# Hybrid decoder layer: gate weights kept for the last pass, output products on VectorE, an earlier reload of h, and a planner that lets short operations go first

## The chip, the cores and the metric

One core of one Trainium2 chip runs the whole layer. The metric is the device time of the execution in microseconds, as the median of several runs. PE is TensorE, DVE VectorE, ACT ScalarE, POOL GpSimd, and SP's queue issues the DMAs.

## The reference

A decoder layer over 1024 tokens of width 1024: an RG-LRU recurrence and a latent attention side by side, an output projection, a SwiGLU feed-forward of width 2816, and a gated per-layer embedding, then a last normalization. The parts that the change touches:

```python
h = h + y @ w_out[l]
vff = rmsnorm(h, g_ffn[l])
h = h + (jax.nn.silu(vff @ w_ffn_gate[l]) * (vff @ w_ffn_up[l])) @ w_ffn_down[l]
e = rmsnorm(p[l] @ w_ple_proj[l], g_ple_post[l])
gate = jax.nn.sigmoid(rmsnorm(h, g_ple_in[l]) @ w_ple_gate[l])
h = h + gate * e
return rmsnorm(h, g_final)
```

## The kernel before

All data is fp32 and transposed: channels lie on the partitions (8 tiles of 128), the 1024 tokens on the free axis. For products a tensor is split into a high and a low fp32r part (`hilo`, `split`, `load_w`: an ACT copy makes the high part, a DVE subtraction the low one), and each product is three matmuls. The feed-forward uses a scheme with seven block products in place of eight (`products`, `PART`), whose sums and differences DVE makes.

The code does not issue instructions as it runs. `Plan` records them; `Plan.order` then plays all engines forward with a table of costs and picks, on each engine that is free, the recorded operation with the smallest key that has its inputs and its buffers. A key is the place in the recording plus shifts (`plan.shift`, `OFF`). Each engine then runs its list strictly in the planned order, so an operation that is late holds all that stand behind it. All instructions are emitted from one line, L364 in the profile.

SBUF is handed out in 51 slots of 128x1024, PSUM in four single banks (`bank`) and two double ones.

The stages, in order: input products and the recurrence (`in_tile`, `rg_front`, `rg_pair`: products `rg`, results `rg_r`, `rg_i`, a scan `rg_h`), attention, the output projection (`wo`), whose result h is kept in DRAM (`hd`). Then 11 pairs of `ff_gate(p)` and `ff_up(p)`, each a block of 84 matmuls of 128x512. `make_x` turns the product of the two into seven hi/lo tiles `hx`, which `spill` stores in DRAM one by one, except for p = 10 (`KEEP`). Then come the down products, in four chunks of the 11 (`CHUNKS`) with four calls of `down` each: `fetch` loads the `hx` tiles back, a call loads two tiles of h in chunk 0, and DVE adds each product to h (`h<-ff_z`, `h<-ff_y`, `h<-ff_x`).

At the end, the embedding products (`ple`), and then the gate products (`gate_mm`, `plg`): 8 tiles n for each of three column ranges h of 512, 256 and 256 tokens (`CH`), 24 matmuls each. `gate_out` evaluates one tile on DVE and ACT (`gt`, `e`, `h`, `o_sq`, `o_acc`), and `out_task` normalizes one column range: transposes `no_ms` and `no_bc`, a short chain on [128, 2 to 4] numbers (`n_m`, `n_rt`, `n_r`, `n_t`), then products of h with `no_rb` and the output DMAs. Each `wpg` weight tile is 512 KB and is loaded and split once for each of the three ranges.

Of the kernel before, what the change touches and what calls it, by code (L numbers as in the profile page):

```python
# [12 lines left out]
ALU = mybir.AluOpType  # L13
# [127 lines left out]
class Plan:  # L141
# [25 lines left out]
    def cost(self, eng, fn, a, k, out):  # L167
        w = out.width() if isinstance(out, View) else 0
        if fn == "dma_start":
            v = k["out"] if isinstance(k["out"], View) else k["in_"]  # L170
            return v.shape[0] * v.width() * 4 / 360e3, 2.1
        if eng == "tensor":
            if fn == "transpose":
                return 0.108, 0.18
            return max(w * 0.000417 + 0.0135, 0.113), 0.18
        if eng == "vector":
            if fn == "reciprocal":
                return 0.065 + w * 0.0063, 0.13
            if fn in ("tensor_reduce", "reduce_sum"):
                return 0.065 + k["in_"].width() * 0.00104, 0.13  # L180
            ptr = 0.061 * any(isinstance(x, View) for x in (k.get("scalar"), *a[2:])) if fn == "scalar_tensor_tensor" else 0.0
            one = fn in ("tensor_copy", "tensor_scalar", "tensor_scalar_mul", "tensor_scalar_add", "tensor_scalar_max")
            if one and all(v.buf.tag not in PS for v in [*a, *k.values()] if isinstance(v, View)):
                return 0.068 + w * 0.00052, 0.13
            return 0.068 + ptr + w * 0.00104, 0.13
        if eng == "scalar":
            src = k["in_"] if "in_" in k else a[1]
            c = (0.052 if src.buf.tag in PS else 0.093) + w * 0.000833
            c += 0.093 * sum(isinstance(k.get(n), View) for n in ("scale", "bias"))
            c += 0.2 * isinstance(k.get("accum_out"), View)  # L190
            return c, 0.14
        return 0.15 + w * (0.0033 if fn == "tensor_copy" else 0.0022), 0.14
# [49 lines left out]
    def order(self):  # L242
# [28 lines left out]
        while left:  # L271
            while frees and frees[0][0] <= t:
                _, _, tag, n = heapq.heappop(frees)
                free[tag] += n
            moved = False
            for e in names:
                while future[e] and future[e][0][0] <= t:
                    _, i, o = heapq.heappop(future[e])
                    heapq.heappush(avail[e], (o.key, i, o))
                if busy[e] > t or not avail[e]:  # L280
                    continue
                pick, skipped, best = None, [], None
                tries = 0
                while avail[e] and tries < 40:
                    i, _, o = heapq.heappop(avail[e])
                    tries += 1
                    ok = all(b.placed or free[b.tag] > min(unplaced(b), RES.get(b.tag, 99)) for b in o.bufs)
                    if ok:
                        key = i
                        if e == "scalar" and o.table and o.table not in SAME.get(table, ()):  # L290
                            key = i + SWITCH
                        if best is None or key < best[0]:
                            if best is not None:
                                skipped.append((best[1], best[2].idx, best[2]))
                            best = (key, i, o)
                        else:
                            skipped.append((i, o.idx, o))
                        if e != "scalar" or key == i:
                            break
                    else:  # L300
                        skipped.append((i, o.idx, o))
                for s in skipped:
                    heapq.heappush(avail[e], s)
                if best is None:
                    continue
                o = best[2]
                moved = True
                start = t
                c = o.cost
                if o.port:  # L310
                    start = max(t, port)
                    port = start + c
                if o.table and o.table not in SAME.get(table, ()):
                    table = FIRST[o.table]
                    c += 1.28
                for b in o.bufs:
                    if b.placed:
                        continue
                    b.placed = True
                    free[b.tag] -= 1  # L320
                    q, d = queue[b.tag], ahead[b.tag]
                    d[b.pos] = True
                    while head[b.tag] < len(q) and d[head[b.tag]]:
                        head[b.tag] += 1
                busy[e] = start + c
                o.end = start + c + o.lat
                o.st = start
                out.append((t, o.idx, o))
                left -= 1
                for b in o.bufs:  # L330
                    b.left -= 1
                    b.done = max(getattr(b, "done", 0.0), start + c + LAT[e, "tensor"] if b.tag in PS and e != "tensor" else o.end)
                    if not b.left:
                        heapq.heappush(frees, (b.done, b.pos, b.tag, 1))
                for s in o.succ:
                    s.npred -= 1
                    r = start + c + (LAT[e, s.eng] if (e, s.eng) in LAT else o.lat)
                    s.ready = max(s.ready, r)
                    if not s.npred:
                        heapq.heappush(future[s.eng], (s.ready, s.idx, s))  # L340
            nxt = [busy[e] for e in names if busy[e] > t and (avail[e] or future[e])]
            nxt += [future[e][0][0] for e in names if future[e] and future[e][0][0] > t]
            if frees:
                nxt.append(frees[0][0])
            nxt = [x for x in nxt if x > t]
            if not left:
                break
            if not nxt:
                raise RuntimeError("the plan does not fit")
            t = min(nxt)  # L350
# [18 lines left out]
FG = ((0, 1), (2, 3), (4, 5), (6, 7))  # L369
TK = 5  # L370
XLATE = 40
NWIDE = 2
PS = ("bank", "wide")
X0 = 0
SWITCH = 150
RES = {'bank': 1, 'slot': 99}


@with_exitstack
def hybrid_layer(ctx, tc, xT, pT, pos, vec, const, const2, w1, wn, wrg, wq, wkv, wo, wg, wu, *rest):  # L380
# [112 lines left out]
    order += [(("wq", 1), wq[1], S)]  # L493
    order += [(("wo", n), wo[n], S) for n in NO]
    order += [(("wpp", k), wpp[k], S) for k in range(2)]
    order += [(("wpg", n, h), wpg[n], S) for h in range(len(CH)) for n in range(8)]
    ready, issued = {}, [0]

    def weight(key, ahead=2):
# [666 lines left out]
    def ff_gate(p):  # L1166
# [3 lines left out]
        def ahead(i):  # L1170
            pump("g", p)
            if i >= 3:
                pump("u", p)
            if p == 0 and i in (0, 3):
                next(nf, None)

# [16 lines left out]
    def ff_up(p, mid):  # L1193
# [3 lines left out]
        def ahead(i):  # L1197
            pump("u", p)
            if i >= 3:
                if p + 1 < NF // 2:  # L1200
                    pump("g", p + 1)
                else:
                    pump("d", 0)
            if p and p - 1 not in KEEP:
                spill(p - 1)
            mid(i)

        def sink(i, ps):
            r, h = PART[i]
# [30 lines left out]
    def fetch(p, i):  # L1240
        t = slot("hx")
        Y.dma_start(out=t, in_=hx[p][i])
        return halves(t.bitcast(F32R))

    def down(c, m, xs, mid, after=None):
        j = 4 * c + m

        def ahead(i):
            pump("d", j)
            if i >= 3:  # L1250
                pump("d", j + 1)
            mid(i)
            if c == 0 and i == 0:
                for n in (2 * m, 2 * m + 1):
                    hs[n] = slot("h")
                    Y.dma_start(out=hs[n], in_=hd[n])

        def sink(i, ps):
            adds = {0: ((0, 0),), 1: ((1, 1),), 2: ((0, 1),), 3: ((0, 1),), 4: ((1, 1),), 5: ((0, 0),), 6: ((1, 0),)}[i]
# [28 lines left out]
    for p in range(NF // 2):  # L1288
        ff_gate(p)
        ff_up(p, (lambda i: first(p - NF // 2 + 4, i)) if p >= NF // 2 - 2 else lambda i: None)  # L1290
    for p in KEEP:
        kept[p] = list(kept[p])


    hg, pacc = [], []
# [43 lines left out]
    ne = rstd_steps(eacc, 1024, "ne", res_)  # L1339
    np_ = rstd_steps(pacc[0], 1024, "np", rps)  # L1340

    def gate_mm(i):
        h, n = divmod(i, 8)
        wh, wl = weight(("wpg", n, h))
        cw = CH[h].stop - CH[h].start
        ps = bank("plg")[:, :cw]
        for k in range(8):
# [7 lines left out]
    def gate_out(i, ps):  # L1355
# [1 line left out]
        cw = CH[h].stop - CH[h].start  # L1357
        t = slot("gt")[:, :cw]
        e, hn = es[n][:, CH[h]], hs[n][:, CH[h]]
        V.scalar_tensor_tensor(out=e, in0=e, scalar=col("g_ple_post", n), in1=res_[0][:, CH[h]],  # L1360
                               op0=ALU.mult, op1=ALU.mult)
        V.tensor_mul(t, ps, rps[0][:, CH[h]])
        A.activation(t, t, AF.Sigmoid)
        if i == 8 * len(CH) - 1:
# [16 lines left out]
    def out_task(h):  # L1381
        res = []
        yield from rstd_part(oaccs[h], 1024, "no", res, h < len(CH) - 1)
        if h < len(CH) - 1:
            for n in range(8):
                hn = hs[n][:, CH[h]]
                G.tensor_mul(hn, hn, res[0])
                Y.dma_start(out=out[n][:, CH[h]], in_=hn)
            return
        cw = CH[h].stop - CH[h].start  # L1390
# [117 lines left out]
```

## Time and profile before

| | |
|---|---|
| median of 3 runs | 1209.58 us (1207.53 to 1210.05) |
| the profiled execution | 1206.05 us |
| its span, first to last instruction | 1204.2 us |
| PE busy | 1164.7 us, 97% |
| DVE busy | 985.5 us, 82% |
| ACT busy | 645.5 us, 54% |
| POOL busy | 250.8 us, 21% |
| mean granted TensorE clock | 0.992 of full speed |

Busy shares are means over stages with different limits. With PE at 97% most of the time can't be moved by an order of instructions; what can is the time in which PE waits, and the time after its last product. A row of the timeline gives the start, the duration, the engine, the operation with out<-in, and in brackets the idle time before it and what ended it. Durations of successive rows overlap a little: the step from start to start is the cost in a row of them.

### The profile page before, as it was taken

The page shows a single profiled execution, that of the slowest core. Times are in us where ns is not written, and L with a number is a line of the kernel's source. Part 1 is how long each engine was busy: PE and PEld are TensorE (multiplying, and loading weights), DVE is VectorE, ACT ScalarE, POOL GpSimd, SP SyncE. Part 2 cuts the span into 40 slices and gives each one's busy share as a digit, 9 for nine tenths or more (in the row PEclk, how much of TensorE's full clock was granted, in tenths as well). Part 3 has the DMA queues.
Part 4 walks back from the last instruction along what each step waited for, and adds up shares of the span by engine and source line. Part 5 has one row for each costly group of instructions (what it writes and reads, how often), then busy time and mean ns, then how long its engine had stood idle before and what let it go on. Part 6 is the DMA issues. An engine that isn't in the chain of part 4 may idle for free.

```text
span 1204.2 us, 15416 instructions
## 1 busy us (share of the span) xinstructions
PE 1164.7 (97%) x5608; PEld 965.5 (80%) x5608; DVE 985.5 (82%) x1486; ACT 645.5 (54%) x1086; POOL 250.8 (21%) x149
## 2 busy tenths in 40 slices
PE   8999999999999999999999999999899999999995
PEld 6788778888878878888888888887687878887894
DVE  7978788888978599988788788876997658776997
ACT  8447868877936354545444454434332214476565
POOL 0001131412102132333213331233000000343042
PEclk9999999999999999999999999999999999999997
DMA  8001100000405142344443445463978773032362
GB/s 339 19 18 35 36 1 1 1 1 1 149 10 192 71 140 71 140 175 161 154 144 136 175 140 175 158 227 146 382 268 283 256 265 133 25 131 88 105 215 84
DMA packets 48252, 158.01 MB, mean 131 GB/s; under 512 B 5424, under 2 KB 8752, under 8 KB 48176
## 3 DMA queue, kind: packets, MB, share of 16 engines
q1 hardware_dynamic: 48176, 157.02, 36.2%
q8 instruction: 44, 0.72, 0.2%
q14 instruction: 32, 0.26, 0.1%
HBM read 111.91 MB, written 45.09 MB: 130 GB/s over the span
## 4 chain that ended last, share of the span: by engine, by line
PE 82%; DVE 10%; ACT 3%; issue 2%; DMA 2%; SPq 0%; DVEq 0%; ACTq 0%
PE ff_z L364 28%; PE ff_y L364 14%; PE ff_x L364 7%; PE plg L364 6%; PE wo L364 5%; PE s L364 4%; PE wn L364 4%; PE av L364 2%; PE tp L364 2%; PE qps L364 2%; DMA wd_r<-in_wd 2%; PE wn_b L364 1%; DVE h L364 1%; PE wn_a L364 1%; PE wo_a L364 1%
## 5 line engine op out<-in xcount | busy, mean ns | idle before, releaser
L364 POOL TENSOR_TENSOR silu<-silu,nf_rb 128x512 f32<-128x512 f32 x77 | 121.5, 1599 | 279.5 <-DVE silu L364 222.0
L364 PE MATMUL ff_z<-hx,wd 128*128 128x512 f32 x528 | 129.8, 393 | 6.1 <-DVE h L364 5.2
L364 PE MATMUL ff_z<-x,wg 128*128 128x512 f32 x528 | 128.5, 391 | 0.2 <-DVE x L364 0.2
L364 PE MATMUL ff_z<-x,wu 128*128 128x512 f32 x528 | 127.1, 390 | 0.9 <-ACT ff_u L364 0.9
L364 PEld LDWEIGHTS ff_z<-hx,wd 128*128 128x128 f32 x528 | 99.4, 189 | 28.7 <-DVE h L364 6.3
L364 PEld LDWEIGHTS ff_z<-x,wu 128*128 128x128 f32 x528 | 99.0, 188 | 22.1 <-ACT ff_u L364 1.4
L364 PEld LDWEIGHTS ff_z<-x,wg 128*128 128x128 f32 x528 | 98.6, 188 | 22.1 <-DVE x L364 0.9
L364 ACT ACTIVATE wd<-wd_r 128x256 fp32r<-128x256 f32 (+2 forms) x64 | 30.0, 492 | 66.5 <-DMA wd_r<-in_wd 28.1
L364 PE MATMUL ff_y<-hx,wd 128*128 128x512 f32 x264 | 65.4, 390 | 0.0
L364 PE MATMUL ff_y<-x,wg 128*128 128x512 f32 x264 | 64.3, 390 | 0.7 <-ACT x L364 0.7
L364 POOL TENSOR_TENSOR p_acc<-p_acc,sq 128x1024 f32<-128x1024 f32 x7 | 18.2, 2595 | 221.4 <-ACT sq L364 221.3
L364 PE MATMUL ff_y<-x,wu 128*128 128x512 f32 x264 | 63.4, 389 | 0.0
L364 DVE TENSOR_TENSOR h<-ff_z,h 128x512 f32<-128x512 f32 x64 | 44.1, 689 | 23.0 <-PE ff_z L364 22.6
L364 PE MATMUL plg<-hg_h,wpg_l 128*128 128x256 f32 (+1 forms) x192 | 61.5, 320 | 1.3 <-DVE wpg_l L364 1.2
L364 PE MATMUL plg<-hg_h,wpg_h 128*128 128x256 f32 (+1 forms) x192 | 61.5, 320 | 0.3 <-ACT np_rb L364 0.3
L364 PE MATMUL plg<-hg_l,wpg_h 128*128 128x256 f32 (+1 forms) x192 | 61.2, 319 | 0.0
L364 ACT ACTIVATE wu<-wu_r 128x512 fp32r<-128x512 f32 x44 | 27.6, 627 | 59.2 <-DVE wu_r L364 28.1
L364 PEld LDWEIGHTS ff_y<-x,wg 128*128 128x128 f32 x264 | 49.4, 188 | 11.5 <-ACT x L364 1.1
L364 PEld LDWEIGHTS ff_y<-hx,wd 128*128 128x128 f32 x264 | 49.8, 189 | 10.5
L364 PEld LDWEIGHTS ff_y<-x,wu 128*128 128x128 f32 x264 | 49.6, 188 | 10.3
L364 ACT ACTIVATE wd<-wd_s 128x256 fp32r<-128x256 f32 (+2 forms) x48 | 23.6, 499 | 63.1 <-DVE wd_s L364 47.8
L364 DVE TENSOR_REDUCE nm<-s 128x1 f32<-128x128 f32 (+3 forms) x64 | 48.1, 752 | 8.7 <-PE s L364 8.1
(407 smaller groups left out, 3060.1 us busy)
## 6 DMA issues: line engine op xcount, KB each, us to landing
hx<-hx SPq DMA_DIRECT2D x140, 512.0 KB, 4.1
wpg_raw<-in_wpg SPq DMA_DIRECT2D x24, 512.0 KB, 3.5
wg_r<-in_wg SPq DMA_DIRECT2D x22, 512.0 KB, 5.5
wu_r<-in_wu SPq DMA_DIRECT2D x22, 512.0 KB, 4.9
wn_raw<-in_wn SPq DMA_DIRECT2D x10, 512.0 KB, 7.1
wo_raw<-in_wo SPq DMA_DIRECT2D x8, 512.0 KB, 4.6
h<-in_xT SPq DMA_DIRECT2D x8, 512.0 KB, 4.4
hd<-h SPq DMA_DIRECT2D x8, 512.0 KB, 2.9
```

The costliest lines, as they stand in the source:

```text
L364: getattr(self.engines[o.eng], o.fn)(*a, **k)
```

## The change

- `order` gets a rule, `HOLD`: on an engine other than PE, where a short operation (cost under 0.25) with a key smaller by over 20 becomes ready within 0.15 us and before the picked operation would end, the engine is left idle until then.
- The planner's cost of `tensor_tensor_scan` on DVE is doubled.
- `spill(p - 1)` is called in `ff_gate(p)`, where it was called in `ff_up(p)`.
- The keys of the `make_x` operations of p = 10 are raised by `KLATE` = 100.
- `reload_h`: the first two tiles of h are loaded in the last `ff_up`, before its sixth product, and those of m + 1 in `down` of m before its fourth, where each was loaded at the start of its own `down`.
- The `wpg` tiles n = 4 to 7 are kept in SBUF from the second column range for the third (`HELD`), with 4 fewer loads and splits.
- `e * g_ple_post * res_` is made once over 1024 columns, where it was made in three pieces.
- The products of h with `no_rb` of the first two column ranges go from POOL to DVE.

```diff
@@ -176,6 +176,8 @@
+            if fn == "tensor_tensor_scan":
+                return 0.068 + w * 0.0021, 0.13
@@ -302,6 +304,12 @@
+                soon = next((r for r, _, x in future[e][:6] if r < t + HOLD and r + 0.05 < t + best[2].cost
+                             and x.cost < 0.25 and x.key + 20 < best[0]), None) if e != "tensor" else None
+                if soon is not None:
+                    heapq.heappush(avail[e], (best[1], best[2].idx, best[2]))
                     continue
@@ -369,10 +377,15 @@
+HOLD = 0.15
+KLATE = 100
+HL = 5
+HAT = 3
+HELD = 4
@@ -493,7 +506,7 @@
-    order += [(("wpg", n, h), wpg[n], S) for h in range(len(CH)) for n in range(8)]
+    order += [(("wpg", n, h), wpg[n], S) for h in range(len(CH)) for n in range(8) if h < 2 or n < HELD]
@@ -1171,6 +1184,8 @@
             pump("g", p)
             if i >= 3:
                 pump("u", p)
+            if p and p - 1 not in KEEP:
+                spill(p - 1)
@@ -1201,9 +1216,9 @@
-            if p and p - 1 not in KEEP:
-                spill(p - 1)
             mid(i)
+            if p == NF // 2 - 1 and i == HL:
+                reload_h(0)
@@ -1242,6 +1257,11 @@
+    def reload_h(m):
+        for n in (2 * m, 2 * m + 1):
+            hs[n] = slot("h")
+            Y.dma_start(out=hs[n], in_=hd[n])
@@ -1250,10 +1270,8 @@
-            if c == 0 and i == 0:
-                for n in (2 * m, 2 * m + 1):
-                    hs[n] = slot("h")
-                    Y.dma_start(out=hs[n], in_=hd[n])
+            if c == 0 and i == HAT and m < 3:
+                reload_h(m + 1)
@@ -1288,8 +1306,10 @@
+    plan.shift = KLATE
     for p in KEEP:
         kept[p] = list(kept[p])
+    plan.shift = 0
@@ -1339,9 +1359,14 @@
+    held = {}
     def gate_mm(i):
         h, n = divmod(i, 8)
-        wh, wl = weight(("wpg", n, h))
+        wh, wl = held[n] if h == 2 and n >= HELD else weight(("wpg", n, h))
+        if h == 1 and n >= HELD:
+            held[n] = wh, wl
@@ -1357,8 +1382,9 @@
-        V.scalar_tensor_tensor(out=e, in0=e, scalar=col("g_ple_post", n), in1=res_[0][:, CH[h]],
-                               op0=ALU.mult, op1=ALU.mult)
+        if h == 0:
+            V.scalar_tensor_tensor(out=es[n], in0=es[n], scalar=col("g_ple_post", n), in1=res_[0],
+                                   op0=ALU.mult, op1=ALU.mult)
@@ -1384,7 +1410,7 @@
-                G.tensor_mul(hn, hn, res[0])
+                V.tensor_mul(hn, hn, res[0])
```

DVE at the change into the down products, before. `hx`, `vt` and `silu` are the parts of p = 10 that `make_x` makes, `h<-ff_z` and `h<-ff_y` the first sums into h:

```order
L364 TENSOR_TENSOR vt<-silu,vt 128x512
L364 TENSOR_TENSOR silu<-silu 128x512
L364 TENSOR_TENSOR hx<-silu,hx 128x512
L364 TENSOR_TENSOR hx<-vt,hx 128x512
L364 TENSOR_TENSOR hx<-silu,hx 128x512
L364 TENSOR_TENSOR silu<-silu,vt 128x512
L364 TENSOR_TENSOR h<-ff_z,h 128x512
L364 TENSOR_TENSOR h<-ff_y,h 128x512
```

The same place with the change; `silu<-ff_z,silu` is the last sum of the last up product:

```order
L372 TENSOR_TENSOR silu<-ff_z,silu 128x512
L372 TENSOR_TENSOR wd_r_7393<-wd_r_7393 128x256
L372 TENSOR_TENSOR wd<-wd_s,wd 128x256
L372 TENSOR_TENSOR h<-ff_z,h 128x512
L372 TENSOR_TENSOR wd<-wd_r_7393,wd 128x256
L372 TENSOR_TENSOR wd_s<-wd_r_7393,wd_r_7386 128x256
L372 TENSOR_TENSOR h<-ff_y,h 128x512
L372 TENSOR_TENSOR hx<-silu,hx 128x512
L372 TENSOR_TENSOR wd<-wd_s,wd 128x256
L372 TENSOR_TENSOR h<-ff_z,h 128x512
```

The operations of p = 10 no longer stand in a row ahead of the first sum into h, but between the later ones.

DVE ahead of the last gate product, before; the products with `no_rb` are on POOL there:

```order
L364 TENSOR_TENSOR gt<-plg,np_rb 128x256
L364 TENSOR_TENSOR e<-gt,e 128x256
L364 TENSOR_TENSOR h<-h,e 128x256
L364 TENSOR_TENSOR e<-gt,e 128x256
L364 TENSOR_TENSOR o_acc<-o_acc,o_sq 128x256
L364 TENSOR_TENSOR h<-h,e 128x256
```

With the change, the same engine at this place:

```order
L372 TENSOR_TENSOR gt<-plg,np_rb 128x256 x2
L372 TENSOR_TENSOR e<-gt,e 128x256 x2
L372 TENSOR_TENSOR h<-h,e 128x256
L372 TENSOR_TENSOR h<-h,no_rb 128x256 x2
L372 TENSOR_TENSOR o_acc<-o_acc,o_sq 128x256
L372 TENSOR_TENSOR h<-h,no_rb 128x256 x6
L372 TENSOR_TENSOR h<-h,e 128x256
```

Eight products of the second column range now stand in DVE's own list, ahead of the last tiles of the third; the eight of the first range stand in a row some 37 operations earlier.

DVE in the recurrence, before, up to the two halves of `zg` that free the PSUM banks `wn_a` and `wn_b`; `rg_h<-rg_r,rg_i` is the scan:

```order
L364 TENSOR_TENSOR rg_i<-rg_i,rg_t 128x1024 x2
L364 SCALAR_TENSOR_TENSOR rg_h<-rg_r,rg_i 128x1024 x2
L364 TENSOR_TENSOR rg_h<-rg_h,zg 128x1024
L364 TENSOR_TENSOR wq_l<-wq_raw,wq_h 128x1024
L364 TENSOR_TENSOR zg<-wn_a,nx_rb 128x512
L364 TENSOR_TENSOR zg<-wn_b,nx_rb 128x512
```

With the change:

```order
L372 SCALAR_TENSOR_TENSOR rg_h<-rg_r,rg_i 128x1024
L372 TENSOR_TENSOR xc<-rg_r 128x1024
L372 TENSOR_TENSOR rg_h<-rg_h,zg 128x1024
L372 SCALAR_TENSOR_TENSOR rg_t<-xc,rg_t 128x1024
L372 TENSOR_TENSOR rg_h<-rg_h,zg 128x1024
L372 TENSOR_TENSOR wq_l<-wq_raw,wq_h 128x1024
L372 TENSOR_TENSOR zg<-wn_a,nx_rb 128x512
L372 TENSOR_TENSOR rg_i<-rg_i,rg_t 128x1024
L372 TENSOR_TENSOR zg<-wn_b,nx_rb 128x512
L372 SCALAR_TENSOR_TENSOR rg_h<-rg_r,rg_i 128x1024
```

The two channels of the pair are no longer worked on side by side: one scan stands ahead of `zg`, the other behind it.

## Rows read from the trace of the kernel before

**Rows 1.** The page, part 1: busy us, share of the span, instructions.

```profile
PE 1164.7 (97%) x5608; PEld 965.5 (80%) x5608; DVE 985.5 (82%) x1486; ACT 645.5 (54%) x1086; POOL 250.8 (21%) x149
```

**Rows 2.** Waits of PE: total us, times, longest us.

```profile
PE no_ms L364 <- DVE o_acc L364: 6.7, 1, 6.7
...
PE ff_z L364 <- DVE h L364: 5.2, 2, 4.2
...
PE kps L364 <- DVE zg L364: 2.0, 1, 2.0
PE plg L364 <- DVE wpg_l L364: 1.2, 2, 0.7
...
PE nx_bc L364 <- DVE q L364: 0.5, 1, 0.5
```

**Rows 3.** Timeline of PE at the change into the down products.

```profile
852.02 1.52 PE L364 MATMUL ff_x<-hx,wd 128*128 128x512 f32 x6
857.70 2.93 PE L364 MATMUL ff_z<-hx,wd 128*128 128x512 f32 x6 [4.15 <-DVE h L364]
860.42 1.63 PE L364 MATMUL ff_y<-hx,wd 128*128 128x512 f32 x6
```

**Rows 4.** Timeline of DVE at the same place.

```profile
850.94 0.69 DVE L364 TENSOR_TENSOR vt<-silu 128x512 f32<-128x512 f32 x1
...
856.35 0.69 DVE L364 TENSOR_TENSOR silu<-silu,vt 128x512 f32<-128x512 f32 x1
856.95 0.69 DVE L364 TENSOR_TENSOR h<-ff_z,h 128x512 f32<-128x512 f32 x1
```

**Rows 5.** Timeline of SP's queue at the same place.

```profile
835.75 10.95 SPq L364 DMA_DIRECT2D hx<-hx  x9
846.80 1.62 SPq L364 DMA_DIRECT2D h<-hd  x2
```

**Rows 6.** Timelines of POOL and DVE in the last two column ranges.

```profile
1154.55 12.94 POOL L364 TENSOR_TENSOR h<-h,no_rb 128x512 f32<-128x512 f32 x8 [59.73 <-ACT no_rb L364]
1185.83 6.83 POOL L364 TENSOR_TENSOR h<-h,no_rb 128x256 f32<-128x256 f32 x8 [18.34 <-ACT no_rb L364]
...
1154.56 1.56 DVE L364 TENSOR_TENSOR h<-h,e 128x256 f32<-128x256 f32 x1
...
1168.93 1.22 DVE L364 TENSOR_TENSOR wpg_l<-wpg_raw,wpg_h 128x1024 fp32r<-128x1024 f32 x1
1170.07 0.42 DVE L364 TENSOR_TENSOR o_acc<-o_acc,o_sq 128x256 f32<-128x256 f32 x1
1170.40 0.42 DVE L364 TENSOR_TENSOR h<-h,e 128x256 f32<-128x256 f32 x1
...
1187.67 0.95 DVE L364 TENSOR_TENSOR o_acc<-o_acc,o_sq 128x256 f32<-128x256 f32 x1
...
1192.00 0.41 DVE L364 TENSOR_TENSOR gt<-plg,np_rb 128x256 f32<-128x256 f32 x1
```

**Rows 7.** Timeline of PE: the first and the last two of 384 gate products of 256 columns.

```profile
1138.32 0.28 PE L364 MATMUL plg<-hg_h,wpg_h 128*128 128x256 f32 x1
...
1187.67 0.28 PE L364 MATMUL plg<-hg_l,wpg_h 128*128 128x256 f32 x1
1187.79 0.28 PE L364 MATMUL plg<-hg_h,wpg_l 128*128 128x256 f32 x1
```

**Rows 8.** Timelines of DVE and PE in the recurrence.

```profile
143.80 4.47 DVE L364 TENSOR_TENSOR_SCAN rg_h<-rg_r,rg_i 128x1024 f32<-128x1024 f32 x2
...
151.27 0.47 PE L364 MATMUL kps<-ckv_h,wkv_h 128*128 128x512 f32 x1 [2.04 <-DVE zg L364]
```

**Rows 9.** Groups by line, of ACT.

```profile
L364 ACT ACT_TABLE_LOAD x25 | 32.1, 1283 | 1.1 <-PEq L1495 0.7
```

**Rows 10.** Windows of a gate block, all instructions; then, of the up block behind it, the tile `hx` alone.

```profile
543.20:562.24 19.04, 19.04 (x86) 15.77 (x85) 15.25 (x23) 9.44 (x17) 5.32 (x4) 1.00 0.52 193
...
562.24:581.28 19.04, 0.00 (x0) 0.00 (x0) 2.46 (x2) 0.05 (x1) 1.00 0.29 111
```

More of the change, by code (lines that the diff above doesn't have):

```diff
@@ L305, in order @@
                     continue
+                soon = next((r for r, _, x in future[e][:6] if r < t + HOLD and r + 0.05 < t + best[2].cost
+                             and x.cost < 0.25 and x.key + 20 < best[0]), None) if e != "tensor" else None
+                if soon is not None:
+                    heapq.heappush(avail[e], (best[1], best[2].idx, best[2]))
+                    continue
                 o = best[2]
```

## The prediction

> **What bounds the kernel.** I read the page first. PE is busy for 1164.7 of 1204.2 us [rows 1], so 39.5 us are open at most: what PE waits for, and the tail after its last product. The change leaves every product of PE in place. I therefore went through the waits of PE, which name what is to be won [rows 2]: 6.7 us ahead of the last `no_ms` transposes, 5.2 us for DVE's sum into h in the down products (one wait of 4.2 us, and 1.0 us elsewhere), 2.0 us ahead of `kps`, 1.2 us for split gate weights, 0.5 us ahead of `nx_bc`. Then came the timeline of each of these places on PE, on the engine it waits for, and on SP.
>
> At the change into the down products PE has three short products done at 853.5 us and stands until 857.70 us [rows 3]: the PSUM bank of `ff_z` is not yet added to h. DVE isn't idle then. It works off ten rows from 850.94 to 856.35 us, 0.60 us apart, nine of them `make_x` of p = 10 and one the last sum of the up product, and takes the sum into h up at 856.95 us [rows 4]. Nobody needs these `hx` parts before chunk 1 (`CHUNKS`). The wait costs more than its length: the six products behind it took 2.93 us, where six took 1.52 us ahead of it [rows 3].
>
> At the end DVE is the bound, not PE. A 128x256 operation of DVE that reads two SBUF tensors takes 0.42 us alone; it took 1.56 us beside POOL's eight 128x512 products and 0.95 us beside the eight of 128x256 [rows 6]. DVE falls behind, PE gets split weights late, and the last product has ended at 1188.07 us when DVE comes to its `gt` only at 1192.00 us [rows 6, 7].
>
> **The change, part by part.** The sum is made in the profiled execution, 1206.05 us with a span of 1204.2 us. The median of the runs, 1209.58 us, lies 3.5 us above it; I take the gain off the median.
>
> *New order at the change into the down products.* With the raised keys the sum into h stands two weight operations behind the last sum of the up product, and the nine operations go between later sums. That removes 4.15 us of waiting and 2.93 - 1.52 = 1.41 us of slow products: 5.6 us. The nine operations, 5.4 us at 0.60 us, move into chunk 0, whose 28 products of up to 1.52 us take some 40 us [rows 3]. What is late next is the data: two tiles of h and the `hx` tiles. Before, SP needed 10.95 us for nine `hx` transfers, stores of p = 9 among them, and came to the first loads of h at 846.80 us [rows 5]. With the change the seven stores of p = 9 stand well ahead, in the gate block, since `spill` is called there; the loads of h have the same neighbours and should issue earlier. Bounds: 0 if the h tiles or weights land as late as DVE was, 5.6 if all are there. I take 5.6.
>
> *Spills in the gate block.* No operation is added. Before, two of the seven `hx` subtractions of a p are in the up block, 2.46 us on DVE [rows 10]; they move into the gate block, where DVE is busy for 15.25 of 19.04 us [rows 10]. 17.7 us still fit; PE had no wait there to give. Cost 0, covered by 1.3 us a block; the first rival takes the cover away.
>
> *Products with `no_rb` on DVE.* They cost DVE 8 x 0.60 + 8 x 0.33 = 7.4 us (start to start, [rows 4, 6]). They remove the slowing: from 1154.56 to 1192.00 us, 37.4 us, DVE did, counted in its order, 43 operations of 128x256 at 0.33, eight weight splits at 1.14 and seven small ones of 0.2 us, together 24.7 us [rows 6]; the other 12.7 us are contention and some idling. *Held weights* take away four splits, 4.6 us on DVE, and four loads. *`e` in one piece* replaces 24 operations, at least 8 x (0.60 + 2 x 0.33) = 10.1 us, by eight of 1024 columns, which this tile hasn't: 9.1 us at the 1.14 us of a split, 18 us at twice that. I take the lower, the same columns with fewer starts, so 0; all of it lies in the first column range, ahead of the stretch counted next.
>
> So with the change DVE has, counted in its order from its first product with `no_rb` to the last `gt`: 50 x 0.33 + 8 x 0.60 + 4 x 1.14 + 1.4 = 27.3 us. PE needs from 1154.5 us on: 384 products from 1138.32 us at 0.12 us apart are 46.1 us, and 12 transposes of at most 0.12 us some 1.3 us, which puts the last one at 1185.6 us instead of 1187.79 us [rows 7]. That leaves 31 us for 27.3 us of DVE. PE is the bound again. Two terms follow. First PE's own 2.2 us. The last three weight tiles now stand on SP behind all eight 256 KB output DMAs of the first range, where before they alternated; they are released by DVE's products, and I expect their split parts about 1 us late. I take 1.2 us, the size of the present wait for weights [rows 2], bounds 0 and 2.2. Second the tail: the last `gt` can start about 0.3 us behind the last product, which in the times of before would be 1188.4 and not 1192.00 us, and from `gt` to the end nothing changes. That is 3.6 us; the lower bound is 1.5 us, if the eight products of 128x256 (2.6 us) stand where the contention of about eight operations (8 x 0.53 = 4.2 us, [rows 6]) stood.
>
> *Planner's costs and the hold rule.* Two scans took 4.47 us [rows 8], which the planner had at half; `zg`, which frees the banks for `kps`, stood behind them, and PE waited 2.04 us [rows 8]. Now one scan stands ahead of `zg` and PE has input products to do ahead of `kps`: 2.0 us, bounds 0 and 2.0. The chain of small operations of the first normalization, which had weight splits between its links, now runs in one piece, three splits earlier: 0.5 us of the wait for `nx_bc` [rows 2], bounds 0 and 0.5. Elsewhere the rule moves operations that PE doesn't wait for, and can leave an engine idle by 0.15 us a time: 0.
>
> The recurrence now switches ACT's tables three times more often, 28 loads in all. At the 1283 ns of the rows [rows 9] that is 3.8 us on ACT, which is busy 54% [rows 1]; hidden by PE's input products, and up to 3.8 us if not. The Trainium skill, page "ScalarE: Activation LUTs", section "What ACT_TABLE_LOAD costs", speaks against the change here: a switch is to cost a drain of about 1.38 us on top, about 2.66 us in all, so by that page the estimate for three is 8.0 us, and the gain would shrink to 5 if all of it lay on the path. The 1283 ns of the rows agree with the page's figure for the load alone.
>
> The sum: 5.6 + 1.2 + 3.6 + 2.0 + 0.5 = 12.9 us. That gives 1193.2 us for an execution like the profiled one and 1209.6 - 12.9 = 1196.7 us for the median.
>
> **The rivals.**
>
> *DVE overflows in the gate blocks (slower).* The `hx` operations that move into the gate block meet POOL's products there. If the seven subtractions of a block grow by what the operations at the end grew beside the smaller products, 0.53 us each, that adds 3.7 us: 17.7 + 3.7 = 21.4 us against 19.04, 2.4 us a block, 24 us over the ten blocks that spill, 1209.6 - 12.9 + 24 = 1221 us. It decides from 1.3 us a block on, where it eats the gain. For it: the two that ran in the up block took 1.23 us each, about twice the 0.69 us of a lone row [rows 4, 10]. Against it: POOL's time is alike in either block, and five of seven are in the gate block already, within the 15.25 us. The Trainium skill, page "SBUF — State Buffer", section "SBUF: two separate sides", has the port that VectorE and GpSimd share as an exclusive lock, held for a whole instruction; by it this rival is likelier than a shared bandwidth would make it. The 0.42 us that became 1.56 us beside POOL agree with it.
>
> *The stall at the change only changes its name.* The first sum into h waits for the tiles of h or `hx`. For it: nine transfers in 10.95 us ahead of these loads [rows 5]. Against: seven stores fewer stand there. No gain there: 12.9 - 5.6 = 7.3, 1202.3 us.
>
> *The end stays DVE's or becomes the loads'.* PE's term falls to 0 and the tail to 1.5: 12.9 - 1.2 - 2.1 = 9.6, 1200.0 us. For it: output DMAs ahead of the last weights, eight products ahead of the last tiles. Against: 31 us for 27.3 us.
>
> *More comes.* PE's whole 2.2 us at the end, the other 1.0 us for h, and runs that lie where the profiled execution does: 1206.1 - 14.9 = 1191.2 us.
>
> **The numbers.** Chances: forecast 0.55 (its own range 1193 to 1199), more 0.08, stall renamed 0.12, end 0.10, overflow 0.15. An overflow near 1.3 us a block leaves the time as it was; a measurement of this kernel tells about 0.2%, 2.4 us, from no change (its runs span 2.5 us). So overflow splits into 0.06 same and 0.08 slower, and 0.01 still faster: faster 0.86, same 0.06, slower 0.08. The range goes from just below "more", 1190.5, to stall and end together, 12.9 - 5.6 - 3.3 = 4.0, 1205.5; it leaves the overflow out. The predicted time is 1196.7 us.
>
> **What would show it.** In the changed profile: PE's wait for DVE's h at the first down product gone or under 1 us, and no clock drop behind it; in the gate blocks PE without idle time and DVE under 19 us; no POOL row of `h<-h,no_rb`, and every 128x256 row of DVE at 0.42 us in the last 50 us; the last `gt` under 0.5 us behind the last product; 28 table loads and no 2.0 us wait ahead of `kps`. The prediction is wrong if PE has idle time in the gate and up blocks, if the first down product waits for a DMA, or if the last gate weights hold PE for over 2 us.

## The result, and the profile after

The median of four runs is 1192.34 us (1192.11 to 1197.23), that of four runs of the kernel before beside them 1209.09 us (1207.53 to 1210.05). The ratio is 0.9872 with a 95% interval of 0.9845 to 0.9900: faster by 1.3%. The profiled execution took 1192.32 us, with a span of 1190.5 us against 1204.2.

The page of the changed kernel, part 1, and its list of PE's waits (total us, times, longest us):

```profile
PE 1161.9 (98%) x5608; PEld 964.9 (81%) x5608; DVE 983.7 (83%) x1482; ACT 646.4 (54%) x1085; POOL 234.9 (20%) x133
```

```profile
PE no_ms L372 <- ACT h L372: 3.0, 1, 3.0
...
PE ff_z L372 <- ACT wd L372: 1.7, 1, 1.7
PE v L372 <- DVE v L372: 1.6, 1, 1.6
PE s L372 <- ACT pB L372: 1.4, 2, 1.2
PE ff_z L372 <- DVE h L372: 1.2, 1, 1.2
...
PE plg L372 <- ACT wpg_h L372: 0.3, 1, 0.3
```

Beside [rows 2]: the wait ahead of `no_ms` fell from 6.7 to 3.0 us, and the 4.2 us for h, `kps` and `nx_bc` are gone. Longer by over half a microsecond are `v` (0.5 before) and `s` (not there before), both in the attention, and `ff_z` for split `wd` weights (0.9 before), far inside the down products.

The changed kernel's PE at the change into the down products, to be held against [rows 3]:

```profile
846.32 1.52 PE L372 MATMUL ff_z<-hx,wd 128*128 128x512 f32 x6
847.68 1.52 PE L372 MATMUL ff_y<-hx,wd 128*128 128x512 f32 x6
849.04 1.54 PE L372 MATMUL ff_z<-hx,wd 128*128 128x512 f32 x6
850.42 1.52 PE L372 MATMUL ff_y<-hx,wd 128*128 128x512 f32 x6
```

Product follows product without a wait. DVE at the same place, against [rows 4], takes the first sum into h up 1.85 us behind the start of the first down product, where it was 7.65 us (849.30 to 856.95 us):

```profile
846.90 0.68 DVE L372 TENSOR_TENSOR silu<-ff_z,silu 128x512 f32<-128x512 f32 x1
...
848.17 0.68 DVE L372 TENSOR_TENSOR h<-ff_z,h 128x512 f32<-128x512 f32 x1
```

At the end DVE, against [rows 6], has every 128x256 row at 0.42 us; the products with `no_rb` stand in its own list:

```profile
1146.96 4.90 DVE L372 TENSOR_TENSOR h<-h,no_rb 128x512 f32<-128x512 f32 x8
...
1172.17 2.09 DVE L372 TENSOR_TENSOR h<-h,no_rb 128x256 f32<-128x256 f32 x6
...
1178.49 0.42 DVE L372 TENSOR_TENSOR gt<-plg,np_rb 128x256 f32<-128x256 f32 x1
```

PE's first and last gate products of 256 columns, against [rows 7]:

```profile
1130.38 0.28 PE L372 MATMUL plg<-hg_h,wpg_h 128*128 128x256 f32 x1
...
1178.17 0.28 PE L372 MATMUL plg<-hg_h,wpg_l 128*128 128x256 f32 x1
```

The last product ends at 1178.45 us and the last `gt` starts at 1178.49; before, 3.93 us lay between them.

In a gate block and the up block behind it (windows: length, then busy us of PE, PEld, DVE, ACT and POOL, granted clock, DMA), against [rows 10], PE has no idle time and DVE is busy for 18.24 of 19.04 us:

```profile
541.75:560.79 19.04, 19.04 (x86) 15.77 (x85) 18.24 (x26) 10.22 (x20) 6.47 (x5) 1.00 0.62 238
560.79:579.83 19.04, 19.04 (x86) 15.77 (x85) 14.37 (x20) 7.41 (x13) 4.96 (x3) 1.00 0.18 66
```

All 21 blocks from the first up block to the last take 399.93 us, 19.04 each; before they took 401.46 us.

### The profile page after: what moved, and what is told of

Its sections match the earlier page's. It is cut to its first block, busy times and chain, and to the rows that moved or that the text cites. A ratio compares the mean times of both kernels' runs of the same rounds, so it can differ in the third digit from the quotient of the medians.

```text
span 1190.5 us, 15414 instructions
## 1 busy us (share of the span) xinstructions
PE 1161.9 (98%) x5608; PEld 964.9 (81%) x5608; DVE 983.7 (83%) x1482; ACT 646.4 (54%) x1085; POOL 234.9 (20%) x133
## 4 chain that ended last, share of the span: by engine, by line
PE 83%; DVE 9%; ACT 4%; DMA 2%; issue 2%; SPq 0%; DVEq 0%; ACTq 0%
PE ff_z L372 29%; PE ff_y L372 14%; PE ff_x L372 7%; PE wo L372 5%; PE plg L372 4%; PE s L372 4%; PE wn L372 4%; PE av L372 2%; PE tp L372 2%; PE qps L372 1%; PE wn_b L372 1%; PE wn_a L372 1%; DVE h L372 1%; DMA wd_r<-in_wd 1%; PE wo_a L372 1%
## 5 line engine op out<-in xcount | busy, mean ns | idle before, releaser
L372 ACT ACTIVATE hx<-silu 128x512 fp32r<-128x512 f32 x55 | 34.6, 629 | 71.3 <-DVE silu L372 42.1
L372 ACT ACTIVATE wd<-wd_r 128x256 fp32r<-128x256 f32 (+2 forms) x64 | 29.9, 491 | 60.2 <-DMA wd_r<-in_wd 21.4
L372 ACT ACTIVATE silu<-silu 128x512 f32<-128x512 f32 x44 | 27.8, 632 | 53.4 <-POOL silu L372 52.9
```

What stands on the lines that cost most here:

```text
L372: getattr(self.engines[o.eng], o.fn)(*a, **k)
```

## The experiments

The times of one kernel differ by up to 5 us from one execution to the next (1192.11 to 1197.23 us with the change), as much as some edits are worth. So the runs are compared by stretches of the profiled execution, cut at starts of PE's products: **A** from the start to the first `wo<-yr`; **B** from there to the first product of the first up block; **C** from there to the first product into `ple` (those into `ple_a` and `ple_b` start 2.7 us earlier); **D** from the first gate product of 256 columns to the end. Between C and D lie 67.9 us in every run. Clock is the granted clock from 352 to 390 us, inside B. All times in us.

| run | A | B | clock | C | D | span | median | ratio, 95% |
|---|---|---|---|---|---|---|---|---|
| before | 322.87 | 124.97 | 0.96 | 622.56 | 65.88 | 1204.2 | 1209.09 | |
| the change | 320.88 | 125.51 | 0.96 | 616.10 | 60.12 | 1190.5 | 1192.34 | 0.9845 to 0.9900 |
| e10 | 321.07 | 125.15 | 0.97 | 623.96 | 59.95 | 1198.0 | 1199.83 | 0.9909 to 0.9941 |
| e4 | 321.50 | 127.29 | 0.91 | 620.14 | 60.10 | 1196.9 | 1196.98 | 0.9859 to 0.9920 |
| e3 | 322.64 | 127.28 | 0.91 | 616.29 | 59.92 | 1194.0 | 1193.38 | 0.9837 to 0.9889 |
| e5 | 321.63 | 124.55 | 1.00 | 615.36 | 60.28 | 1189.7 | 1191.54 (one run) | |
| e11 | 321.28 | 124.46 | 1.00 | 616.22 | 60.54 | 1190.4 | 1194.53 | 0.9863 to 0.9900 |
| e12 | 321.31 | 125.29 | 0.96 | 623.21 | 60.12 | 1197.8 | 1200.00 | 0.9914 to 0.9944 |
| e8 | 323.18 | 124.49 | 1.00 | 624.58 | 61.47 | 1201.6 | 1204.36 | 0.9943 to 0.9975 |
| e1 | 322.64 | 125.66 | 0.96 | 617.13 | 62.79 | 1196.1 | 1196.52 | 0.9877 to 0.9907 |
| e2 | 321.12 | 124.52 | 1.00 | 615.71 | 61.66 | 1190.9 | 1192.44 | 0.9843 to 0.9876 |
| e6 | 323.04 | 125.42 | 0.96 | 615.87 | 60.95 | 1193.2 | 1194.96 (one run) | |
| e7 | 323.26 | 124.92 | 0.96 | 616.26 | 60.18 | 1192.5 | 1194.28 (one run) | |
| e13 | 321.50 | 124.54 | 1.00 | 617.10 | 60.68 | 1191.7 | 1192.96 | 0.9853 to 0.9891 |

How to read it: B follows the clock (124.5 us at 1.00, 124.9 to 125.7 at 0.96 to 0.97, 127.3 at 0.91). What repeats tells the grain: C lies between 615.4 and 617.1 us in all runs with the spill in the gate block, and between 622.6 and 624.6 in the three with the whole old change into the down products (before, e10, e8); D lies between 59.9 and 60.7 in those with its whole new end, apart from e6.

### The change into the down products

**e10** undoes all three edits at this place: the spill's place, the keys and the loads of h.

```diff
-KLATE = 100
+KLATE = 0
@@ ff_gate
-            if p and p - 1 not in KEEP:
-                spill(p - 1)
@@ ff_up
+            if p and p - 1 not in KEEP:
+                spill(p - 1)
-            if p == NF // 2 - 1 and i == HL:
-                reload_h(0)
@@ down
-            if c == 0 and i == HAT and m < 3:
-                reload_h(m + 1)
+            if c == 0 and i == 0:
+                reload_h(m)
```

> The change with its three parts for the down products undone together (keys of p = 10 not raised, spills in the up block, h loaded at the start of its own down); the end and the planner's rules stay. If the gain at the change into the down products is due to these parts, PE's wait of about 4 us for DVE's sum into h is back, with slow products behind it, and the time is 5 to 7 us above the change. If the hold rule or the shifted order ahead of it made it, the wait stays under 1 us and the time within 1 us.

C came back to 623.96 us, and with it the wait of 3.9 us for h and the 0.8 us for `ff_u`. So this place is worth 7.9 us here and 6.5 from before to the change, and the other stretches don't depend on it. With the same old order at this place, C of e8 is 2.0 us longer than that of before; the granted clock from 856 to 866 us was 0.66 in e8 and 0.83 in before.

**e4** undoes the spill's place alone (the lines of e10's diff on `spill`).

> The change with the spills back in the up block; raised keys and early loads of h stay. Theory A: two operations of p = 10 ahead of the sum, so the wait is 0 to 1.5 us and the time within 1.5 us of the change. Theory B: the loads of wd stand behind the stores of p = 9 on SP again, DVE waits 2 to 3.5 us for the weights, PE 2 to 4 us for DVE, and the time is 3 to 5 us above the change.

C was 620.14 us, 4.0 more than with the change: the price of theory B. DVE waited 3.27 us for the weights, as it says, but PE only 1.64 us for DVE, less than its 2 to 4.

**e3** undoes the keys alone (`KLATE = 0`).

> The change with the keys of p = 10 not raised; its list on DVE has eight operations of p = 10 in a row ahead of the first sum into h again, while spills and loads of h stay as in the change. Theory A (the order on DVE made the wait): PE waits 3 to 4.5 us for the sum into h, slow products behind it cost 1.4 us, the time is 4 to 6 us above the change. Theory B (DVE was late because stores of p = 9 held the loads of wd on SP, and DVE waited 3.4 us for them; the order only passed it on): the wait is 0 to 1.5 us and the time within 2 us of the change.

C was 616.29 us, 0.2 more, with a wait of 1.13 us for the sum into h. The 3.5 us of its span over the change's are A and B, where this edit has no operation, and the clock is 0.91. The theory of the prediction, that the keys make the gain, falls.

**e5** undoes the early loads of h alone (the lines of e10's diff on `reload_h` and those around them).

> The change with h loaded at the start of its own down. Theories A and B: the loads have nearly the same neighbours on SP, PE's wait for the sum into h stays under 1 us, span within 1 us of the change. Rival (h must be there early): PE waits 1 to 3 us for h in one or more of the first four downs, span 1 to 4 us above.

C was 615.36 us, 0.7 less than with the change: in this one run they are worth nothing beside the new spill.

Since each edit might stand in for another, two more runs take one edit alone. **e11** has the spill in the gate block, and the keys and loads as before:

```diff
-KLATE = 100
+KLATE = 0
@@ ff_up
-            if p == NF // 2 - 1 and i == HL:
-                reload_h(0)
@@ down
-            if c == 0 and i == HAT and m < 3:
-                reload_h(m + 1)
+            if c == 0 and i == 0:
+                reload_h(m)
```

> The change with KLATE = 0 and the old loads of h, so that of the three edits at the change into the down products the spill's place alone is left. Measured from the first product of the first up block to the first ple product: 622.6 us before, 616.1 us with the change, 616.3 us with KLATE = 0, 624.0 us with all three undone. Theory A (the place of the spill is enough): 615.5 to 617 us, no wait of ff_z for ff_u, at most 1.5 us for h at the first down products. Theory B (the keys or the early loads are needed beside it): 619 us or more, a wait of about 4 us for h.

**e12** has the raised keys, with the spill in the up block and the old loads (e10's diff without the lines on `KLATE`):

> The change with the spill back in the up block and the old loads of h, so that of the three edits the raised keys alone are left. Same stretch as in the run with the spill alone. Theory A (the keys are a second cure of the wait for h, and the early loads do nothing): 619.5 to 621 us, as with the spill undone alone (620.1 us), with the waits for ff_u (0.8 us) and for h (1.6 us). Theory B (the keys need the early loads, since the first sum into h waits for its tile): 622 us or more, the wait of DVE or PE at the first sum 3 us or longer and put down to the load of h.

C was 616.22 us with the spill alone, the whole gain, and 623.21 us with the keys alone, next to none. Windows of PE in e12 and then in e11, in the 20 us from 846 us on:

```profile
846.00:866.00 20.00, 16.65 (x66) 13.28 (x66) 18.79 (x38) 8.17 (x18) 0.00 (x0) 0.91 1.02 412
```

```profile
846.00:866.00 20.00, 18.86 (x84) 15.27 (x83) 20.00 (x43) 7.06 (x16) 0.00 (x0) 1.00 0.76 282
```

With the keys alone PE idles for 3.35 us of these and the granted clock is 0.91 in the mean; with the spill alone it idles for 1.14 us, and the clock is full. The DMA engines are busy for 1.02 of the window in e12 and for 0.76 in e11. Theory A of e12 is refuted too: the keys cure nothing without the early loads, and e4 (620.14) against e12 (623.21) says that with the old spill and the raised keys the early loads are worth 3.1 us.

What the spill's place has to do with DVE's lateness can be read on SP. In the kernel before, whose last up block starts at 828.86 us, SP's queue does this:

```profile
829.05 0.32 SPq L364 DMA_DIRECT2D hx<-hx  x1
833.91 0.32 SPq L364 DMA_DIRECT2D hx<-hx  x1
834.28 0.42 SPq L364 DMA_DIRECT2D wd_r<-in_wd  x1
834.80 0.38 SPq L364 DMA_DIRECT2D hx<-hx  x1
835.27 0.38 SPq L364 DMA_DIRECT2D wd_r<-in_wd  x1
```

The second transfer stands for 4.5 us. It loads an `hx` tile into a slot that a `silu` of POOL still holds, as the waits of SP from 828.9 to 834.5 us say:

```profile
SPq L364 <- POOL silu L364: 3.9, 1, 3.9
```

Behind it stand the two loads of `wd`, with a store of p = 9 between them. ACT of the same kernel then waits for them, and DVE, whose next operation is their split, idles for 3.38 us:

```profile
839.36 0.42 ACT L364 ACTIVATE wd<-wd_r 128x256 fp32r<-128x256 f32 x1 [3.26 <-DMA wd_r<-in_wd]
839.81 0.42 DVE L364 TENSOR_TENSOR wd<-wd_r,wd 128x256 fp32r<-128x256 f32 x1 [3.38 <-ACT wd L364]
```

From there on ACT is late with its copy `ff_u`, which stands behind in its list (0.94 us of PE), and DVE with p = 10 and with h. The wait of 3.9 us for POOL's `silu` is in e4, e8, e10 and e12 too, all with the spill in the up block, and so is DVE's idle time (3.2 to 3.4 us). In the changed kernel and in e11, where p = 9 is stored earlier, SP doesn't wait for POOL ahead of these loads (the changed kernel waits 0.4 us for it behind them), and the changed kernel has both `wd` loads issued within 1.9 us from 830.04 us on, 2.8 us behind the start of its last up block, where it was 5.4:

```profile
830.04 1.86 SPq L372 DMA_DIRECT2D wd_r<-in_wd  x2
```

A second path goes through the same queue. The first sum also needs its tile of h. Before, the loads of h issue at 846.80 us [rows 5] and take 8.7 us to land, as the list of DMA issues from 840 to 860 us has it (number, size, median us to landing):

```profile
h<-hd SPq DMA_DIRECT2D x6, 512.0 KB, 8.7
```

So the tile is there at about 855.5 us, and a DVE in time could have begun the sum only some 1.4 us ahead of its 856.95 us. In e4, where keys and early loads leave DVE ahead of the tile, it does wait for it:

```profile
855.17 0.69 DVE L372 TENSOR_TENSOR h<-ff_z,h 128x512 f32<-128x512 f32 x1 [0.36 <-DMA h<-hd]
```

In e11, with the old loads in the code, the same loads issue 10.2 us ahead of the first down product (at 845.67 us), where it was 2.5, and the weights of the next `down` behind them at 836.36 us, where it was 848.53:

```profile
835.52 0.79 SPq L372 DMA_DIRECT2D h<-hd  x2
836.36 0.92 SPq L372 DMA_DIRECT2D wd_r<-in_wd  x2
```

The spill's place also spreads the transfers. Two windows of before and the one of the changed kernel at the place of the first:

```profile
820.00:830.00 10.00, 10.00 (x46) 8.26 (x45) 5.74 (x9) 3.73 (x7) 7.18 (x5) 1.00 0.29 107
850.00:860.00 10.00, 5.85 (x22) 4.44 (x21) 9.51 (x17) 5.04 (x10) 0.00 (x0) 0.86 1.03 414
```

```profile
818.00:828.00 10.00, 10.00 (x46) 8.29 (x45) 8.98 (x9) 3.90 (x7) 6.12 (x5) 1.00 0.65 249
```

Before, the DMA engines have a share of 0.29 ahead of the last up block and are full (1.00 to 1.03) from 840 to 870 us, where h is to land. With the change they are full from 838 to 858 us (1.02 and 0.99), but the first two tiles of h were issued at 833.74 us.

That the spill's place does it is shown by e11. That it does so through slots (the stores give those of p = 9 back) and SP's queue is read from these rows; no run freed a slot in another way. For h there is one hint: from e12 to e4, both with the old spill and the raised keys, its loads issue 4.8 us ahead of the first down product and not 2.5, and C is 3.1 us shorter, while DVE still waits 3.27 us for the `wd` weights. No run brought these weights alone earlier, so how the 7.7 us fall to DVE's late weights, to h and to the full DMA engines stays open.

### The end

**e8** takes the kernel before, and only puts its products with `no_rb` on DVE; **e1** takes the changed kernel and puts them back on POOL.

```diff
-                G.tensor_mul(hn, hn, res[0])
+                V.tensor_mul(hn, hn, res[0])
```

> The kernel before with one edit: the sixteen products with no_rb on DVE. Theory: every 128x256 row of DVE in the last 50 us is at 0.42 us, PE's last 384 gate products take 48 to 48.5 us from start to start (49.5 before), the tail is 12.5 to 14.5 us, and the time 3 to 5 us below before. Rival (DVE is full and the moved products go on its path): no gain, or up to 3 us above before.

> The change, but with the sixteen products of h with no_rb back on POOL; held weights, one-piece e and all else stay. Theory (POOL slows DVE's two-tensor operations, and that alone made the tail): DVE rows beside POOL are at 0.9 to 1.5 us again, from the start of the last gate product to the end it takes 14.5 to 16.5 us (12.3 in the change, 16.4 before), and the time is 3 to 6 us above the change. Rival (the four held weight tiles unloaded DVE, and the place of the products hardly counts): 12.3 to 13.3 us from the last gate product to the end, and the time within 1.5 us of the change.

D fell by 4.4 us in e8 (65.88 to 61.47) and rose by 2.7 in e1 (60.12 to 62.79). DVE of e1 beside POOL's eight products, which ran from 1177.14 us for 6.71 us:

```profile
1177.23 0.42 DVE L372 TENSOR_TENSOR gt<-plg,np_rb 128x256 f32<-128x256 f32 x1
1177.56 0.63 DVE L372 TENSOR_TENSOR e<-gt,e 128x256 f32<-128x256 f32 x1
1178.12 0.96 DVE L372 TENSOR_TENSOR o_acc<-o_acc,o_sq 128x256 f32<-128x256 f32 x1
1179.00 0.96 DVE L372 TENSOR_TENSOR h<-h,e 128x256 f32<-128x256 f32 x1
```

The slowing is back, in the operations with two inputs in SBUF, and not in `gt`, which reads one from PSUM. The Trainium skill, page "SBUF — State Buffer", section "SBUF: two separate sides", has the shared port taken by VectorE only with two SBUF inputs (or in a faster mode); the trace agrees, with 0.42 us for the one and 0.96 for the other.

The price in e1 was below the expected one, and 1.2 us of it is not contention. From the last `gt` to `no_ms` it takes 2.75 us before (1192.00 to 1194.75), 2.91 in the changed kernel (1178.49 to 1181.40), but 4.1 us in e8 and e2, and in e1 from the second of its last two `gt`. ACT of e2, with the table load ahead of the last square:

```profile
1178.73 1.28 ACT L372 ACT_TABLE_LOAD   x1
1180.03 0.20 ACT L372 ACTIVATE warm<-gt 128x1 f32<-128x1 f32 x1
1180.14 0.40 ACT L372 ACTIVATE o_sq<-h 128x256 f32<-128x256 f32 x1
```

In the changed kernel ACT's last square stands ahead of the load (and the last of all is on DVE):

```profile
1178.17 0.40 ACT L372 ACTIVATE o_sq<-h 128x256 f32<-128x256 f32 x1
1178.61 0.51 ACT L372 ACTIVATE h<-h,vc 128x256 f32<-128x256 f32 x1
1179.02 0.40 ACT L372 ACTIVATE gt<-gt 128x256 f32<-128x256 f32 x1
1179.44 1.28 ACT L372 ACT_TABLE_LOAD   x1
```

**e2** loads and splits all eight weights again in the third range.

```diff
-HELD = 4
+HELD = 8
```

> The change with no held weights (all eight tiles loaded and split again in the third column range). Theory (contention was the cost): DVE gets 4.6 us of splits back and has about 32 us of work for PE's 31, so the tail grows by 0.5 to 2 us and the time by 0.5 to 2.5 us. Rival (the held weights made the gain at the end): the tail is back at 15 us or more and the time 3 us or more above the change.

D was 61.66 us, 1.5 more than with the change; the total, 1192.44 us, hides it, since A and B were 0.75 us shorter and C 0.4. Of the 1.5 us, 1.2 are the place of the table load. By that reading the held weights themselves are worth 0.3 us, and the products on DVE alone would have made the whole gain at the end (e8: 65.88 - 61.47 + 1.2 = 5.6 of 5.8 us). No run had the old loads of the weights together with the good place of the table load, so this split is worked out, not shown, and 0.3 us is less than the grain of D.

### The planner's two edits

**e6** sets the hold rule to nothing, **e7** gives the scan its old cost back.

```diff
-HOLD = 0.15
+HOLD = 0.0
```

> The change with the hold time set to 0 (no engine is left idle for a short operation). Theory: the rule gave the 0.5 us ahead of nx_bc and little else, so the wait at nx_bc comes back with about 0.5 us and the span is 0 to 1.5 us above the change. Rival (the rule carries the gain at kps, too): span 2 to 4 us above.

```diff
-            if fn == "tensor_tensor_scan":
-                return 0.068 + w * 0.0021, 0.13
```

> The change with the planner's old cost of the scan; the hold rule stays. Theory A (the scan's cost gives nothing in the end): the wait ahead of kps is back at about 2.0 us and kps starts 2 us later than the 146.78 us of the change, but the waits of v (1.58 us) and of s (1.43 us), which came with the new order, go back to about 0.5 and 0, so that the first output product on yr starts within 0.6 us of the 320.88 us of the change. Theory B (the gain at kps is kept): it starts about 2 us later, at 322.9 us, as in the kernel before (322.87 us).

Without the hold rule the span was 2.7 us above the change's, in the rival's range. Both waits ahead of `nx_bc` were back (0.5 and 0.7 us), that at `kps` was not, though `kps` started 2.4 us later (149.17 us). A was 323.04 us at full clock, where the seven runs with both edits whose clock was full from 147 to 320 us lie between 320.88 and 321.63, 321.26 in the mean: the rule is worth 1.8 us there, and 0.8 in D, which is little over the grain. e7 did not settle the scan: its A of 323.26 us holds a stretch at a clock of 0.98 (147 to 240 us), as the 322.64 us of e1 and e3 do, and those are the 1.5 us in question. Its waits went as theory A has it: `kps` 2.0 us, `v` 0.5, none at `s`.

**e13** leaves out both the early loads and the scan's cost (the diffs of e7 and e5).

> The change without two of its edits that gave nothing so far: the early loads of h and the cost of the scan. Theory (both are worth nothing): within 1.5 us of the change in span once the clock behind the output projection is alike, that is 1188 to 1193 us, 0.985 to 0.989 of the kernel before. Rival (one of them carries part of the gain): 1194 us or more.

At full clock its A was 321.50 us, with the wait of 2.0 us at `kps` in it. So the scan's cost is worth 0.2 us, which is nothing: what it gains at `kps`, `v` and `s` give back. The kernel without these two edits runs as the change does (1192.96 us, 0.9853 to 0.9891); no version here was measurably faster.

## Why the prediction was right, and where it was not

Before to after, the profiled spans differ by 13.7 us; the forecast sum was 12.9. By its terms:

- **Change into the down products, 5.6 forecast, 6.5 measured** (C). The wait and the slow products went as said; later waits for `wd` and h grew by 1.0 us, which leaves 4.9 us from the first down product to `ple`. The other 1.5 us lie ahead of it, the wait for `ff_u` and the slow products behind it, which the prediction didn't see. **The failed step is the cause**: "With the raised keys the sum into h stands two weight operations behind". The keys alone give 0.8 us at most (e12 against e10), less than the grain. The spill's move, priced as "Cost 0" for what it adds to the gate block, makes the gain, 7.7 us alone (e10 to e11). The prediction had read SP's queue for the loads of h and expected them earlier by this very move, but only as what the keys' gain needs. It didn't see the first `wd` weights, which stand there 12 us earlier, and took DVE's ten rows in a row for a matter of order, where DVE was late before they began. The size came out near because the term was the length of the wait, whatever removes it: as to its cause that is luck. The rival of a stall for h or `hx` did not come in the changed kernel; e4 comes nearest to it.
- **Gate blocks, 0 forecast.** Held: PE 19.04 of 19.04 us, DVE 18.24 where 17.7 was worked out. The rival of an overflow, at 21.4 us, did not come; the cover left is 0.8 us.
- **PE's last gate products, 1.2 forecast, 1.7 measured** (49.75 to 48.07 us from the first of 256 columns to the last); the wait for weights is 0.3 us.
- **Tail, 3.6 forecast, 4.1 measured** (16.13 to 12.05 us). The mechanism held in both directions (e8, e1). Held weights, counted among DVE's savings, were hardly needed.
- **Recurrence, 2.5 forecast, 1.6 to 2.0 measured** (322.87 us to the mean of 321.26, and to 320.88). `kps` started 4.5 us earlier, more than forecast, and 2.5 us of it went to `v` (1.58 us for 0.48) and `s` (1.43). The prediction priced waits and did not ask what the earlier `kps` would wait for next. The scan's cost takes the wait at `kps` away (2.0 us in e7 and e13, none in e6), but is worth 0.2 us for 2.0 forecast; the hold rule is worth 1.8 (e6, one run) for 0.5, of which 1.2 are the two waits ahead of `nx_bc`, and the prediction had counted one of them. That their sum came near is luck.
- **Table loads**: 28, as forecast. That they are hidden holds for the recurrence, where no wait of PE from 120 to 160 us is put down to ACT; whether a load has a part in the later wait at `s` no run tells. At the end one of them costs 1.2 us where it stands ahead of a square. The Trainium skill, page "ScalarE: Activation LUTs", section "What ACT_TABLE_LOAD costs", puts 1.38 us of drain on top; in the rows of e2 `warm` starts at 1180.03 us, 1.30 us behind the start of the load, so the trace shows the load and no drain.

The predicted 1196.7 us was 4.4 us too high, and 0.8 of it is the sum. The rest is the base: the gain was taken off the median of before, whose profiled execution (1206.05 us) lies 3.0 us below its median, while that of the change lies at its median. Why the other executions of before are longer has no trace. Their granted clock is on record: of twenty timed beside the experiments, the six at 0.992 or 0.993, like the profiled one's 0.992, took 1208.2 us in the mean, the fourteen with a lower clock 1209.8. So 1.6 us go with the clock, and the rest stays open.

## What to carry to other kernels

When an engine is found working off a row of operations while its consumer waits, follow it back to where it last idled: the order of that row may matter less than what made it late. On a queue that several stages share, a transfer that waits for its buffer holds the next stage's first loads; giving buffers back earlier can be worth more than the order of the work behind, as it was here. One late engine can hide a second late input: here the tile of h landed 1.4 us ahead of the sum that DVE came to late. Edits that bear on one wait should also be tried one at a time, each alone: undoing one at a time left the spill worth 4.0 us, and alone it gave 7.7 (e10 to e11).

## What the runs showed of the hardware

PE's clock behind the output projection differs from run to run at the same order of work. From 352 to 390 us, behind a wait of 2.5 to 2.6 us for `ya_h` that all runs have, the granted clock was 1.00, 0.96 to 0.97 or 0.91 of full speed, a mean over parts at 2.4 GHz and a part at 1.2. Windows of e3 and then of e2:

```profile
352.00:390.00 38.00, 37.17 (x150) 30.12 (x151) 29.82 (x31) 21.90 (x28) 8.05 (x3) 0.91 0.44 152
```

```profile
352.00:390.00 38.00, 37.37 (x165) 30.59 (x164) 32.61 (x35) 21.07 (x27) 8.22 (x3) 1.00 0.44 152
```

Both have PE busy for the 37 us, with 150 records against 165; B was 127.28 and 124.52 us. These 2.8 us are a fifth of the 13.7 us between the profiled executions of before and the change, and belong to no edit.
